# An encoder block on one core: seeded accumulation in two stages of seven-product pairs, normalised-input sums one operation per slot, attention tables in a pool of their own, and new filling counts

## The chip, the core and the metric

The program runs on one core of one Trainium2 chip. The core has a matrix engine (TensorE, "PE" in the profile, with "PEld" for its weight loads), a vector engine (VectorE, "DVE"), an activation engine (ScalarE, "ACT"), GpSimd ("POOL"), and SyncE ("SP"), whose queue here issues the DMAs. Operands lie in SBUF, matrix products accumulate in eight banks of PSUM. The metric is the device time of the program in microseconds; less is better.

## What is computed

The reference is one layer of a hybrid encoder block on 1024 tokens of width 1024, in float32:

```
h = rms_norm(x); proj = h @ w_in            # q,k,v,r, gate codes, swa q,k,v, two branch gates
y_gla = (bidirectional gated linear attention, 4 heads, silu(r) gate) @ w_o_gla
y_swa = (windowed attention, 8 heads, 2 kv heads, rope, sinks) @ w_o_swa
x = x + (sigmoid(gate_a) * y_gla + sigmoid(gate_b) * y_swa) @ w_out
h2 = rms_norm(x); gu = h2 @ w_ffn_in
x = x + (silu(gu[:, :2816]) * gu[:, 2816:]) @ w_ffn_out
```

## The kernel before

Every float32 matrix product is made of three products of rounded operands: a tile is split into a high part (rounded, one ACT operation) and a low part (the rest, one DVE subtraction), and PE runs high x high, high x low and low x high into one bank. The output tiles are 128 x 512, so one "product" of a weight unit (128 x 512) is 4 slices x 3 = 12 matmuls. PE's order is written out by hand (`manual_schedule`); the other engines and the DMA queue are ordered by the compiler's scheduler, on the whole by the order of the program text where operands and buffers are ready.

Dense work that nothing waits for soon is a list of generators, `dense`: the projections of v, q, k (`proj_t`, `proj_f`) and, last in the list, `first_halves`, which makes the first of seven products for twelve pairs of output rows (r, ga and gb, four each). It leaves, for each pair, the product `p1` in DRAM. `fill(n)` takes n matmuls from that list and puts them into PE's order. The stages in between are latency-bound chains, and they run in slots: `slot(stages, n)` issues the stages of one slot with n dense matmuls spread among them. `need(key)` fills on until a projection that a stage reads is done.

- **Linear attention (GLA), slots 0 to 44.** Each slot holds `g_gates` (every other slot), `g_scores`, `g_out`, `g_back_out`, `g_turn` of different chunks. The table `GF` gives n: 34 below slot 8, 21 below 24, 17 below 35, then 10. At the ends of slots 1 to 8, `x_sums` loads tiles of x, normalises them (`x_norm`, line 559) and makes the differences that the second half of the pairs needs (`x_diff`, line 564; `put`, line 116, stores each to DRAM). There are four tiles (`xn`) for these.
- **Windowed attention, slots 0 to 21.** After the pools of GLA are closed, new pools are opened in their place, five tables (cosb, sinb, band, qg, kg) and the sinks are loaded there (line 62 by `load_const`), four tables qA and qB are worked out on DVE (lines 619 to 622), and the slots of `prep`, `a_rope`, `a_scores`, `a_turn`, `k_turn`, `a_out`, `a_probs` run, with n from the table `SF`: 50 below slot 2, 25 below 18, then 15. Line 661 is the load of a key and value tile into the single buffer `kvr`, lines 159 and 167 store and load again the split weights of `proj_t`. Slots 18 to 21 also load and split two parts of the x differences (`xpart`, lines 782, 773, 774).
- **Second half of the pairs.** The last of `dense` is filled in among four `xpart("T2", k)`; then `second_first(0)` (three weight loads, a sum `s1`, its split, the product T1 into the bank Z), eight more `xpart`, and twelve times `second_rest`: products T2, 22, T3, T4 into X and Z. `p1` is loaded (line 869) and added by DVE three times per pair: to Z (line 872, tile p5), to X after T2 (line 877, tile u2), and to X after T4 (in `result`, line 851). Line 830 is a weight load, 835 a weight sum, 821 and 822 the high and low part of a weight.
- **Output projections**, eight-unit groups (`hgroup`), with PE never waiting.
- **Feed-forward, first matrix.** 22 features in `ffn_in`, built like the pairs: `p1` is copied out of PSUM by ACT in `p11`, and added by DVE at line 1106 (p5), 1110 (u2) and 1125 (c21). `between` holds the products of the next feature that stand between T2 and T3.
- **Feed-forward, second matrix** (line 1187), seven products over eleven units with four banks each.

Of the kernel before, what the change touches and what calls it, by code (L numbers as in the profile page):

```python
# [25 lines left out]
GF = ((8, 34), (24, 21), (35, 17), (1 << 30, 10))  # L26
SF = ((2, 50), (18, 25), (1 << 30, 15))
# [5 lines left out]
def body(tc, i, out):  # L33
    nc = tc.nc
    with ExitStack() as root:
# [78 lines left out]
        def put(key, t):  # L114
            d = scratch("_".join(map(str, key)))
            nc.sync.dma_start(out=d, in_=t)
            scr[key] = d

# [435 lines left out]
        part = {}  # L554

# [11 lines left out]
        def x_sums(j):  # L567
            k, late = divmod(j, 2)
            if not late:
                a, b = part[k] = x_norm(k, 0), x_norm(k, 1)  # L570
                x_diff("xT1", k, b, b, a)
                return
            a, b = part.pop(k)
            c = x_norm(k + 4, 1)
            put(("x22", k), c)
            x_diff("xT2", k, b, c, b)
            x_diff("xT3", k, a, b, a)
            c = x_norm(k + 4, 0)
            x_diff("xT4", k, c, c, b)
# [3 lines left out]
        for n in range(NH * NC):  # L583
# [3 lines left out]
            for j, (t, f) in enumerate(((n, g_gates), (n + 2, g_scores), (n + 3, g_out),  # L587
# [3 lines left out]
                last = max(last, t)  # L591
        with tc.manual_schedule(engines={mybir.EngineType.PE}):
            fill(36)
            for t in range(last + 1):
                slot([(lambda v=at[t, j]: v[0](*v[1:])) if (t, j) in at else None for j in (0, 5, 4, 3, 2, 1)], share(GF, t))
                if 1 <= t <= 8:
                    x_sums(t - 1)
# [6 lines left out]
        cosb = load_const(sc_, "cosb", i["c_cos"], (P, KT, 64))  # L604
        sinb = load_const(sc_, "sinb", i["c_sin"], (P, KT, 64))
        band = load_const(sc_, "band", i["c_band"], (P, 384))
        qg = load_const(sc_, "qg", i["qg"], (P, P))
        kg = load_const(sc_, "kg", i["kg"], (P, P))
# [200 lines left out]
        swas.close()  # L809

# [35 lines left out]
        def ntile():  # L846
            return tp.tile([P, HT], F32, tag="nt", name=nm("nt"), bufs=6)
# [8 lines left out]
        def second_first(f):  # L856
            nme, m, a, b = PAIRS[f]
            g = pend[f] = Chunk()
            g.r11, g.r21 = rawload(i["w_f"][a, 0], True), rawload(i["w_f"][b, 0], True)
            g.r22 = rawload(i["w_f"][b, 1], False)  # L860
            g.s1 = comb(g.r21, g.r22, ALU.add)
            g.Z = chtile((P, HT))
            product(g.Z, wsplit(g.s1, 512), XT["T1"], 4, True, False)

        def second_rest(f):
            nme, m, a, b = PAIRS[f]
            g = pend.pop(f)
            p1 = ntile()
            nc.sync.dma_start(out=p1, in_=scr[f"{nme}{m}", "p1"])
            r12 = rawload(i["w_f"][a, 1], False)  # L870
            p5 = ntile()
            nc.vector.tensor_tensor(p5, g.Z, p1, op=ALU.add)
            X = mmtile()
            s2 = comb(g.s1, g.r11, ALU.subtract)
            product(X, wsplit(s2, 512), XT["T2"], 4, True, False)
# [493 lines left out]
```

## Time and profile before

| | |
|---|---|
| median of 3 runs | 1679.72 us (1677.94 to 1680.65) |
| the profiled execution | 1681.57 us, of which 1679.8 us are the span from its first to its last instruction |
| busy share of the span | PE 98%, PEld 81%, DVE 74%, ACT 51%, POOL 0% |
| instructions | 23620, of them 7740 matmuls |
| mean granted clock of PE | 0.993 |
| DMA | 304.32 MB, mean 181 GB/s |

The views used below: the **windows** give, for a stretch of the span, the busy time of each engine with its number of instructions, then the granted clock of PE (1.00 is full), the mean busy share of the DMA engines and GB/s. The **waits** give who waited for whom, with total, number and longest in us. The **groups** give, for a line of code and an operation, the busy time in us, the mean of one in ns, and the idle time of the engine before them with what ended it. The **timeline** gives start, length and, in brackets, the idle time of the engine before and what ended it. `SPq` is the DMA queue of SyncE. The length of a matmul in these rows covers its whole latency; back to back, 512-column matmuls start every 0.227 us (610.06, 610.29, 610.52 in the timeline).

### The profile page before, as it was taken

The page shows a single profiled execution, that of the slowest core. Times are in us where ns is not written, and L with a number is a line of the kernel's source. Part 1 is how long each engine was busy: PE and PEld are TensorE (multiplying, and loading weights), DVE is VectorE, ACT ScalarE, POOL GpSimd, SP SyncE. Part 2 cuts the span into 40 slices and gives each one's busy share as a digit, 9 for nine tenths or more (in the row PEclk, how much of TensorE's full clock was granted, in tenths as well). Part 3 has the DMA queues.
Part 4 walks back from the last instruction along what each step waited for, and adds up shares of the span by engine and source line. Part 5 has one row for each costly group of instructions (what it writes and reads, how often), then busy time and mean ns, then how long its engine had stood idle before and what let it go on. Part 6 is the DMA issues. An engine that isn't in the chain of part 4 may idle for free.

```text
span 1679.8 us, 23620 instructions
## 1 busy us (share of the span) xinstructions
PE 1652.1 (98%) x7740; PEld 1366.0 (81%) x7740; DVE 1250.0 (74%) x2506; ACT 855.2 (51%) x1783; POOL 0.2 (0%) x4
## 2 busy tenths in 40 slices
PE   9989999999999989999999999999999999999999
PEld 7878888887888868888888888788888888888887
DVE  8687887845989777875673668887778877789755
ACT  7445886872897752433553556533333333344443
POOL 0000000000000000000000000000000000000000
PEclk9999999999999999999999999999999999999999
DMA  8875646668654474655764545344224543595533
GB/s 291 292 241 194 213 152 198 220 233 291 202 160 141 126 225 157 225 185 187 237 213 141 192 133 181 114 132 138 89 94 140 165 159 128 178 325 186 150 99 119
DMA packets 185851, 304.32 MB, mean 181 GB/s; under 512 B 21150, under 2 KB 46494, under 8 KB 185728
## 3 DMA queue, kind: packets, MB, share of 16 engines
q1 hardware_dynamic: 185728, 302.81, 55.5%
q8 instruction: 61, 1.00, 0.3%
q14 instruction: 62, 0.51, 0.1%
HBM read 206.26 MB, written 96.47 MB: 180 GB/s over the span
## 4 chain that ended last, share of the span: by engine, by line
PE 81%; DVE 8%; ACT 4%; DMA 4%; issue 2%; SPq 1%; ACTq 0%; DVEq 0%
PE mm L75 25%; PE mm L842 7%; PE mm L843 7%; PE mm L844 7%; PE mm L1187 7%; PE ch L75 6%; PE ch L1187 5%; PE ch L842 4%; PE ch L843 4%; PE ch L844 4%; PE mm L242 3%; PE ch L750 1%; DVE wl L71 1%; DVE cs L418 1%; DMA xr<-in_xT_dram 1%
## 5 line engine op out<-in xcount | busy, mean ns | idle before, releaser
L821 ACT ACTIVATE wh<-ws 128x512 fp32r<-128x512 f32 x136 | 85.5, 632 | 182.5 <-PE mm L843 103.1
L69 ACT ACTIVATE wh<-wr 128x512 fp32r<-128x512 f32 x190 | 118.4, 628 | 103.8 <-PE mm L75 71.3
L71 DVE TENSOR_TENSOR wl<-wr,wh 128x512 fp32r<-128x512 f32 x190 | 129.8, 686 | 26.0 <-ACT wh L69 25.5
L75 PE MATMUL mm<-wh,xh 128*128 128x512 f32 x320 | 128.4, 401 | 1.2 <-DMA wh<-wh 1.1
L75 PE MATMUL mm<-wl,xh 128*128 128x512 f32 x320 | 128.5, 402 | 0.9 <-DMA wl<-wl 0.9
L75 PE MATMUL mm<-wh,xl 128*128 128x512 f32 x320 | 127.7, 399 | 0.0
L822 DVE TENSOR_TENSOR wl<-ws,wh 128x512 fp32r<-128x512 f32 x136 | 93.0, 685 | 12.5 <-ACT wh L821 12.4
L821 ACT ACTIVATE wh<-wr 128x512 fp32r<-128x512 f32 x64 | 40.4, 632 | 114.3 <-issue 47.9
L821 ACT ACTIVATE wh<-a 128x512 fp32r<-128x512 f32 x66 | 41.7, 632 | 92.9 <-PE ch L1187 42.3
L822 DVE TENSOR_TENSOR wl<-a,wh 128x512 fp32r<-128x512 f32 x66 | 45.5, 691 | 41.5 <-ACT wh L821 40.6
L75 PEld LDWEIGHTS mm<-wh,xh 128*128 128x128 f32 x320 | 60.7, 190 | 11.4 <-DMA wh<-wh 1.5
L1187 PE MATMUL mm<-hh,wh 128*128 128x512 f32 x176 | 68.6, 390 | 0.7 <-DVE c L1125 0.7
L75 PEld LDWEIGHTS mm<-wl,xh 128*128 128x128 f32 x320 | 60.7, 190 | 9.9 <-DMA wl<-wl 1.2
L1187 PE MATMUL mm<-hl,wh 128*128 128x512 f32 x176 | 68.5, 389 | 0.0
L1187 PE MATMUL mm<-hh,wl 128*128 128x512 f32 x176 | 68.5, 389 | 0.0
L75 PEld LDWEIGHTS mm<-wh,xl 128*128 128x128 f32 x320 | 60.7, 190 | 9.1
L1160 DVE TENSOR_TENSOR hl<-hr,hh 128x512 fp32r<-128x512 f32 x77 | 52.8, 686 | 3.9 <-ACT hh L1159 3.8
L835 DVE TENSOR_TENSOR ws<-wr,wr 128x512 f32<-128x512 f32 x68 | 46.7, 688 | 8.5 <-DMA wr<-in_w_fi_dram 4.6
L75 PE MATMUL mm<-xh,wh 128*128 128x512 f32 x128 | 51.6, 403 | 0.2 <-ACT wh L69 0.2
L75 PE MATMUL mm<-xl,wh 128*128 128x512 f32 x128 | 51.6, 404 | 0.1
L1187 PE MATMUL ch<-hh,wh 128*128 128x512 f32 x132 | 51.3, 389 | 0.0
L1187 PE MATMUL ch<-hl,wh 128*128 128x512 f32 x132 | 51.3, 389 | 0.0
(546 smaller groups left out, 4986.9 us busy)
## 6 DMA issues: line engine op xcount, KB each, us to landing
wr<-in_w_fi_dram SPq DMA_DIRECT2D x102, 256.0 KB, 2.9
wr<-in_w_f_dram SPq DMA_DIRECT2D x88, 256.0 KB, 3.0
wh<-wh SPq DMA_DIRECT2D x80, 256.0 KB, 2.8
wl<-wl SPq DMA_DIRECT2D x80, 256.0 KB, 3.0
B<-c SPq DMA_DIRECT2D x44, 256.0 KB, 2.1
T<-st SPq DMA_DIRECT2D x44, 256.0 KB, 2.6
a<-in_w_fo_dram SPq DMA_DIRECT2D x44, 256.0 KB, 5.2
hr<-T SPq DMA_DIRECT2D x44, 256.0 KB, 2.6
```

The costliest lines, as they stand in the source:

```text
L69: nc.scalar.activation(h, raw, AF.Copy)
L71: nc.vector.tensor_tensor(l, raw, h.bitcast(F32), op=ALU.subtract)
L75: nc.tensor.matmul(o, a, b, start=start, stop=stop)
L242: nc.tensor.matmul(Y[q], w[:, c], x, start=f0, stop=f1, skip_group_check=True)
L821: nc.scalar.activation(h, src, AF.Copy)
L822: nc.vector.tensor_tensor(l, src, h.bitcast(F32), op=ALU.subtract)
L835: nc.vector.tensor_tensor(t, x, y, op=op)
L842: nc.tensor.matmul(o, h[:, c], x[kk][0], start=start and kk == 0, stop=False, skip_group_check=True)
L843: nc.tensor.matmul(o, h[:, c], x[kk][1], start=False, stop=False, skip_group_check=True)
L844: nc.tensor.matmul(o, l[:, c], x[kk][0], start=False, stop=kk == nk - 1, skip_group_check=True)
L1160: nc.vector.tensor_tensor(l, r, h.bitcast(F32), op=ALU.subtract)
L1187: nc.tensor.matmul(ys[m], a[:, c], b, start=f0, stop=f1, skip_group_check=True)
```

## The change

Six edits, each in the diff below:

1. `GF` has 19 where it had 17 (slots 24 to 34) and 12 where it had 10 (from slot 35). `SF` has 52 for 50 (slots 0 and 1), 24 for 25 (slots 2 to 8), 19 for 25 (slots 9 to 17) and 12 for 15 (slots 18 to 21).
2. `x_sums` is a generator that makes one load with its normalisation, or one difference with its store, at the end of each slot from slot 1 on: 32 steps, done with slot 32.
3. The five tables lie in a pool of their own, `swk`, at the right side of SBUF, opened ahead of GLA and closed after the windowed attention; their loads stand ahead of the slots of GLA. The sinks, qA and qB stay where they were.
4. In the twelve pairs, `p1` is loaded in `second_first` and copied by ACT into the bank X, and T2, T3 and T4 accumulate upon it; T1 goes to a new function `second_go`. What DVE added is now read out by ACT copies: p5 from Z, u2 from X, and the last result from X.
5. `second_first(0)` stands ahead of the third of the four `xpart("T2", k)`, before the last dense matmuls.
6. In the 22 features, `p1` is copied by ACT into X as well; p5 and c21 lose their addition, and u2 is an ACT copy.

```diff
@@ -23,8 +23,8 @@
...
 WARM = 10
-GF = ((8, 34), (24, 21), (35, 17), (1 << 30, 10))
-SF = ((2, 50), (18, 25), (1 << 30, 15))
+GF = ((8, 34), (24, 21), (35, 19), (1 << 30, 12))
+SF = ((2, 52), (9, 24), (18, 19), (1 << 30, 12))
 PAD = 672
@@ -115,6 +115,9 @@
...
             scr[key] = d
+
+        swks = ExitStack()
+        swk = swks.enter_context(tc.tile_pool(name="swk", bufs=1, side="right"))
 
@@ -551,8 +554,6 @@
...
 
-        part = {}
-
         def x_norm(k, s):
@@ -564,19 +565,31 @@
...
 
-        def x_sums(j):
-            k, late = divmod(j, 2)
-            if not late:
-                a, b = part[k] = x_norm(k, 0), x_norm(k, 1)
+        def x_sums():
+            for k in range(KT // 2):
+                a = x_norm(k, 0)
+                yield
+                b = x_norm(k, 1)
+                yield
                 x_diff("xT1", k, b, b, a)
-                return
-            a, b = part.pop(k)
-            c = x_norm(k + 4, 1)
-            put(("x22", k), c)
-            x_diff("xT2", k, b, c, b)
-            x_diff("xT3", k, a, b, a)
-            c = x_norm(k + 4, 0)
-            x_diff("xT4", k, c, c, b)
+                yield
+                c = x_norm(k + 4, 1)
+                put(("x22", k), c)
+                yield
+                x_diff("xT2", k, b, c, b)
+                yield
+                x_diff("xT3", k, a, b, a)
+                yield
+                c = x_norm(k + 4, 0)
+                yield
+                x_diff("xT4", k, c, c, b)
+                yield
+
+        cosb = load_const(swk, "cosb", i["c_cos"], (P, KT, 64))
+        sinb = load_const(swk, "sinb", i["c_sin"], (P, KT, 64))
+        band = load_const(swk, "band", i["c_band"], (P, 384))
+        qg = load_const(swk, "qg", i["qg"], (P, P))
+        kg = load_const(swk, "kg", i["kg"], (P, P))
 
@@ -589,23 +602,19 @@
...
                 last = max(last, t)
+        sums = x_sums()
         with tc.manual_schedule(engines={mybir.EngineType.PE}):
...
                 slot([(lambda v=at[t, j]: v[0](*v[1:])) if (t, j) in at else None for j in (0, 5, 4, 3, 2, 1)], share(GF, t))
-                if 1 <= t <= 8:
-                    x_sums(t - 1)
+                if t:
+                    next(sums, None)
         glas.close()
...
         sw = swas.enter_context(tc.tile_pool(name="swt", bufs=2))
-        cosb = load_const(sc_, "cosb", i["c_cos"], (P, KT, 64))
-        sinb = load_const(sc_, "sinb", i["c_sin"], (P, KT, 64))
-        band = load_const(sc_, "band", i["c_band"], (P, 384))
-        qg = load_const(sc_, "qg", i["qg"], (P, P))
-        kg = load_const(sc_, "kg", i["kg"], (P, P))
         sink = load_const(sc_, "sink", i["sink"], (P, 8))
@@ -807,6 +816,7 @@
...
         swas.close()
+        swks.close()
 
@@ -844,7 +854,7 @@
...
         def ntile():
-            return tp.tile([P, HT], F32, tag="nt", name=nm("nt"), bufs=6)
+            return tp.tile([P, HT], F32, tag="nt", name=nm("nt"), bufs=4)
 
@@ -856,35 +866,44 @@
...
             g = pend[f] = Chunk()
+            p1 = tp.tile([P, HT], F32, tag="np", name=nm("np"), bufs=2)
+            nc.sync.dma_start(out=p1, in_=scr[f"{nme}{m}", "p1"])
+            g.X = mmtile()
+            nc.scalar.copy(g.X, p1)
             g.r11, g.r21 = rawload(i["w_f"][a, 0], True), rawload(i["w_f"][b, 0], True)
...
             g.s1 = comb(g.r21, g.r22, ALU.add)
+            g.w = wsplit(g.s1, 512)
+
+        def second_go(f):
+            g = pend[f]
             g.Z = chtile((P, HT))
-            product(g.Z, wsplit(g.s1, 512), XT["T1"], 4, True, False)
+            product(g.Z, g.w, XT["T1"], 4, True, False)
 
...
             g = pend.pop(f)
-            p1 = ntile()
-            nc.sync.dma_start(out=p1, in_=scr[f"{nme}{m}", "p1"])
+            X = g.X
             r12 = rawload(i["w_f"][a, 1], False)
             p5 = ntile()
-            nc.vector.tensor_tensor(p5, g.Z, p1, op=ALU.add)
-            X = mmtile()
+            nc.scalar.copy(p5, g.Z)
             s2 = comb(g.s1, g.r11, ALU.subtract)
-            product(X, wsplit(s2, 512), XT["T2"], 4, True, False)
+            product(X, wsplit(s2, 512), XT["T2"], 4, False, True)
             u2 = ntile()
-            nc.vector.tensor_tensor(u2, X, p1, op=ALU.add)
+            nc.scalar.copy(u2, X)
             s4 = comb(r12, s2, ALU.subtract)
...
             s3 = comb(g.r11, g.r21, ALU.subtract)
-            product(X, wsplit(s3, 512), XT["T3"], 4, False, False)
+            product(X, wsplit(s3, 512), XT["T3"], 4, False, True)
             result((f"{nme}{m + 4}", 1), X, p5)
...
                 second_first(f + 1)
+                second_go(f + 1)
             product(X, wsplit(g.r22, 512), XT["T4"], 4, False, True)
-            result((f"{nme}{m + 4}", 0), X, p1)
+            t = stage()
+            nc.scalar.copy(t, X)
+            put((f"{nme}{m + 4}", 0), t)
 
@@ -908,10 +927,12 @@
...
             for k in range(4):
+                if k == 2:
+                    second_first(0)
                 xpart("T2", k)
...
             fill(1 << 30)
-            second_first(0)
+            second_go(0)
             for q in ("T3", "T4"):
@@ -1099,19 +1120,19 @@
...
             Z, X = chtile((P, HT)), mmtile()
+            nc.scalar.copy(X, p1)
             s1 = comb(F.r21, F.r22, ALU.add)
...
             nc.scalar.copy(p5, Z)
-            nc.vector.tensor_tensor(p5, p5, p1, op=ALU.add)
             s2 = comb(s1, F.r11, ALU.subtract)
-            product(X, wsplit(s2, 512), YX["T2"], 4, True, False)
+            product(X, wsplit(s2, 512), YX["T2"], 4, False, True)
             u2 = ctile("u2")
-            nc.vector.tensor_tensor(u2, X, p1, op=ALU.add)
+            nc.scalar.copy(u2, X)
             for p, g in between:
...
             s3 = comb(F.r11, F.r21, ALU.subtract)
-            product(X, wsplit(s3, 512), YX["T3"], 4, False, False)
+            product(X, wsplit(s3, 512), YX["T3"], 4, False, True)
             c22 = ctile("c22")
@@ -1122,8 +1143,7 @@
...
             c21, g0 = ctile("c21"), F.g0
-            nc.vector.tensor_tensor(c21, X, p1, op=ALU.add)
-            nc.vector.tensor_tensor(c21, c21, g0, op=ALU.mult)
+            nc.vector.tensor_tensor(c21, X, g0, op=ALU.mult)
             nc.vector.tensor_tensor(c22, c22, u2, op=ALU.mult)
```

## The prediction

> **What bounds the kernel now.** I read the page first, then the windows, the waits of PE stage by stage, and the timeline where PE waits.
>
> ```profile
> PE 1652.1 (98%) x7740; PEld 1366.0 (81%) x7740; DVE 1250.0 (74%) x2506; ACT 855.2 (51%) x1783; POOL 0.2 (0%) x4
> ```
>
> PE is busy for all but 28 us of the span, and no matmul is removed. So the change can gain only where PE waits or runs at a lower clock. The windows say where (span, then busy us of PE, PEld, DVE, ACT, POOL, the granted clock, the share of the DMA engines, GB/s):
>
> ```profile
> 80.00:145.00 65.00, 59.16 (x287) 48.57 (x286) 50.26 (x119) 29.35 (x74) 0.00 (x0) 0.92 0.73 239
> 145.00:260.00 115.00, 114.09 (x662) 97.84 (x661) 94.98 (x270) 88.56 (x255) 0.00 (x0) 1.00 0.56 178
> 260.00:380.00 120.00, 117.20 (x646) 97.10 (x646) 79.29 (x225) 89.00 (x257) 0.00 (x0) 1.00 0.67 223
> 380.00:404.00 24.00, 21.97 (x90) 17.43 (x89) 13.94 (x40) 5.84 (x14) 0.00 (x0) 0.93 0.83 276
> ...
> 477.20:550.50 73.30, 71.71 (x380) 60.56 (x379) 70.45 (x205) 62.60 (x148) 0.00 (x0) 1.00 0.49 154
> 550.50:601.00 50.50, 49.90 (x262) 40.70 (x261) 32.77 (x93) 35.02 (x84) 0.00 (x0) 1.00 0.40 124
> 601.00:627.00 26.00, 19.98 (x78) 15.95 (x77) 20.71 (x33) 15.14 (x26) 0.00 (x0) 0.87 0.84 272
> 627.00:780.00 153.00, 153.00 (x677) 126.60 (x675) 113.73 (x177) 45.84 (x73) 0.00 (x0) 1.00 0.55 183
> ...
> 1076.00:1460.00 384.00, 384.00 (x1695) 318.06 (x1695) 301.77 (x486) 130.86 (x217) 0.00 (x0) 1.00 0.40 131
> ```
>
> Three stretches lose much: the start of GLA (5.84 us idle in 65, and 8% of the clock, 5.2 us), the passage from GLA to the windowed attention (2.03 us, and 7% of 24, 1.7 us), and the passage to the pairs (6.02 us, and 13% of 26, 3.4 us). Together 24 us. In the pairs and the features (627 to 780, 1076 to 1460) PE has no gap, so taking DVE additions away there is worth nothing by itself.
>
> **a. x_sums one operation per slot (80 to 145).** The timeline of DVE at 110, and the groups of the two operations:
>
> ```profile
> 110.83 0.75 DVE L559 SCALAR_TENSOR_TENSOR xn<-xn,g,rstd 128x512 f32<-128x512 f32 x1 [4.12 <-DMA xn<-in_xT_dram]
> ...
> 118.00:124.00 6.00, 3.12 (x13) 1.95 (x12) 6.00 (x16) 3.17 (x9) 0.00 (x0) 0.80 0.31 98
> 124.00:129.00 5.00, 5.00 (x16) 4.09 (x16) 2.58 (x6) 1.66 (x5) 0.00 (x0) 0.56 0.90 289
> L564 DVE TENSOR_TENSOR xn<-xn,xn x16: 669/688/694, 47.0 to 125.5; 128x512 f32<-128x512 f32 x16
> L559 DVE SCALAR_TENSOR_TENSOR xn<-xn,g,rstd x16: 732/748/752, 34.7 to 124.5; 128x512 f32<-128x512 f32 x16
> ```
>
> DVE waits 4.12 us for an x tile, and as it works in order the gates of that slot are late by as much: PE idles 2.88 of the 6 us from 118 and then runs 5 us at 0.56 of its clock. 32 operations (22 us at 0.69 us) with 36 DMAs stand in slots 1 to 8, to about 126 us; now eight stand there. I take 8.5 of the 11.0 us: the residue of 2.5 is more than the next window loses (0.91 in 115), since the slots still hold v's outputs. The ends: 11, and 3 if the DMA waits come back one by one.
>
> **b. The 24 operations that move to slots 9 to 32 (145 to 345).** About 15 of them fall into 145 to 260: 10 us of DVE onto 94.98 of 115, 83% to 91%. Still below full. Nothing if they fill gaps; 10 us if each lies in a gate chain. I take +1.5, nearer to nothing, since DVE has 20 us of gaps there. Their SP work moves with them: 27 of the 36 x-tile DMAs now queue among the loads and stores of these slots, where a store that waits for DVE holds the weight loads behind it; the x loads can run ahead by four buffers.
>
> **c. Two more fills per slot in slots 24 to 44.** 42 matmuls of 0.227 us, in front of stages that leave PE idle for 2.80 us in 260 to 380. That work is not new, it comes from the windowed attention. -1 (from -2.5 to +2, the x operations of slots 24 to 32 included).
>
> **d. Tables early.** The passage at 380:
>
> ```profile
> 384.37 0.43 SPq L661 DMA_DIRECT2D kvr<-skv  x1
> 387.21 0.69 DVE L619 TENSOR_TENSOR qA<-cosb,qg 128x512 f32<-128x512 f32 x1 [11.58 <-DMA kvr<-skv]
> 392.04 0.32 SPq L661 DMA_DIRECT2D kvr<-skv  x1
> 392.40 0.43 SPq L167 DMA_DIRECT2D wh<-wh  x1
> SPq L661 <- DVE qn L636: 3.5, 1, 3.5
> 394.00:398.00 4.00, 1.97 (x8) 1.06 (x8) 4.00 (x7) 0.76 (x3) 0.00 (x0) 1.00 0.97 330
> 398.00:402.00 4.00, 4.00 (x12) 3.15 (x11) 2.97 (x13) 1.74 (x4) 0.00 (x0) 0.57 0.66 224
> ```
>
> The second kvr load waits 3.5 us for DVE to be done with the first tile, and the weight loads of L167 stand behind it in SP's queue; they come too late for PE. With five issues (0.43 us each) gone ahead of the first kvr, and qA and qB worked out before it lands instead of after (four operations, 2.4 us from start to start), the second kvr comes about 4.5 us earlier; PE was short by 2.03. I take -3.5 of 3.7. The sinks stay behind the close of the pools, so the wait for memory stays; if it alone decides, 0. The table loads (5 issues) now stand where PE has 78.52 of 80 us busy at the start; no pool holds them back, and x-tile DMAs leave that stretch by (a). I cost them at nothing; without that cover, up to 2.9 us (0.83 MB at the 292 GB/s of the row below), and this end I keep.
>
> ```profile
> 0.00:80.00 80.00, 78.52 (x357) 61.83 (x358) 61.06 (x114) 48.62 (x86) 0.20 (x4) 1.00 0.86 292
> ```
>
> **e. Fewer fills in the windowed attention.** A 512-column matmul takes 0.227 us from start to start (610.06 and 610.29 under f). From 477 to 550 (slots 9 to 14) DVE is busy 70.45 of 73.30 us: it is as much the bound as PE. Six fills fewer in six slots take 36 x 0.227 = 8.2 us from PE. From DVE they take a split and an output (L71, L245) per 12 matmuls, 3 pairs at 1.2 us by starts, 3.6 us. If DVE keeps its 2.85 us of gaps, the stretch shrinks by 3.6, and 4.6 of the 8.2 us turn into waiting. From 550 on DVE is busy 32.77 of 50.5, and slots 2 to 8 lose one fill each: nothing. +4.6; the ends are 0 and 8.2.
>
> **f. The passage to the pairs.**
>
> ```profile
> L242 PE MATMUL mm<-xh,wh 128*128 128x512 f32 x13 | 5.1, 389 | 0.0
> 610.06 0.39 PE L842 MATMUL ch<-xh,wh 128*128 128x512 f32 x1
> 610.29 0.39 PE L843 MATMUL ch<-xl,wh 128*128 128x512 f32 x1
> 610.98 0.32 SPq L248 DMA_DIRECT2D gb<-st  x1
> 611.58 0.92 SPq L782 DMA_DIRECT2D xn<-xT  x2
> 612.55 0.98 SPq L869 DMA_DIRECT2D nt<-r_p  x1
> 613.59 0.90 SPq L830 DMA_DIRECT2D wr<-in_w_f_dram  x2
> ...
> 619.11 0.69 DVE L835 TENSOR_TENSOR ws<-wr,ws 128x512 f32<-128x512 f32 x1
> 620.48 0.63 ACT L982 ACTIVATE ga<-ga 128x512 f32<-128x512 f32 x1 [2.06 <-DMA ga<-ga]
> 621.68 0.80 PE L842 MATMUL ch<-xh,wh 128*128 128x512 f32 x1 [6.02 <-ACT wh L821]
> ```
>
> After the last attention matmul PE has 3 x 13 = 39 dense matmuls, then T1 and T2; then it waits for the weight s4, whose load (613.59) stands behind the x tiles, `p1`, and the last store of the dense work, and whose split stands behind a gate's sigmoid. By the counts of GF, SF and `need`, slots 20 and 21 and the rest now leave 12 + 12 + 36 = 60. PE has cover for 60 x 0.227 + 24 x 0.227 = 19.1 us after 601, where the split ended about 20.4 us after it (621.0 and 0.6); `p1` is loaded before, and its two additions leave DVE's queue ahead of the sum at 619. (`p1` of every pair is now loaded ahead of the weights of its pair, one load more in front of them at 0.43 us of SP; its bank is taken a product earlier, of four.) I take -7.5 of 9.4. The ends: 9.4, and 0.
>
> **g. Seeds and copies (pairs and features).** Per product pair, DVE loses three additions (0.69 us), ACT gains a seed into PSUM and read-outs: four copies in a pair, two in a feature. No row shows a write into PSUM by ACT; a read from it is
>
> ```profile
> L1105 ACT COPY p<-ch 128x512 f32<-128x512 f32 x22 | 12.5, 567 | 0.0
> L821 ACT ACTIVATE wh<-ws 128x512 fp32r<-128x512 f32 x42 | 26.6, 632 | 65.9 <-PE mm L843 35.2 <-PE ch L843 26.1 <-PE mm L844 2.4
> PE mm L842 <- DVE u L1110: 1.3, 1, 1.3
> ```
>
> I take 0.57 us, the ends 0 and 0.75 (the slowest 128 x 512 row above). ACT has 45.84 us busy of 153 in the pairs and 130.86 of 384 in the features, and four copies add 2.3 us to a pair of 60 x 0.227 = 13.6. Its splits (L821, windows of 627 to 780) wait for PE to free one of five weight buffers, so they run some four products, 10.9 us, ahead: a copy between them costs PE nothing. With that cover gone it would be 0.57 + 0.63 = 1.2 us a pair. The one wait of PE for a DVE read-out, 1.3 us at 1073 behind DVE's queue, goes to an idle ACT: -1.3 (end 0).
>
> **The sum.** -8.5 + 1.5 - 1 - 3.5 + 4.6 - 7.5 - 1.3 = -15.7. The profiled execution took 1681.57 us, 1.77 outside the span; so 1665.9 like for like. It lay 1.85 above the median of the runs, which gives 1664.0 for the median.
>
> One rule against these prices. The Trainium skill, "TensorE: Matmul & The Clock Gate", section "HAM oscillation — how this bites in real kernels", has the clock fall after idle gaps of more than about 3.4 us. By it the gaps of PE before 600 would draw no low clock of their own. The trace disagrees: in 394 to 398 PE was busy 1.97 of 4 us in several pieces, and 0.57 followed.
>
> **The rivals.**
> 1. *The wait for s4 stays.* If the load of s4 still stands behind the last dense store, that store moves later with the 21 more matmuls, and the wait with it. For: 610.98 stands 0.9 us after the last dense matmul. Then f gives 1: 1670.5. Chance 0.15.
> 2. *DVE is the bound in GLA too.* b costs 8, a gives 5: 1674. For: 83% before; against: 20 us of gaps. 0.08.
> 3. *All given back*: b costs 8, e its end of 8.2, f gives 1, the rest as taken: -8.5 + 8 - 1 - 3.5 + 8.2 - 1 - 1.3 = +0.9, 1680.6: no change. The stalls only move to where less filling stands. 0.07.
> 4. *The low clock is not owed to the short gaps* and falls as before: the 5.2 and 1.7 us of a and d stay: 1664.0 + 6.9 = 1671. The rows at 118 and 394, where it follows the gaps, speak against it. 0.04.
> 5. *Slower: ACT's queue.* ACT works in order; if the copy u2, which waits for the end of T2, stands ahead of the split of the weight that PE needs next, PE waits 1.2 us in each of 12 + 22 products: +40.8, 1705. It decides once the lead of the splits falls below one product, 2.7 us. Against: the lead of four. 0.06.
> 6. *All better*: a, d and f whole, e at nothing: 1664.0 - 2.5 - 0.2 - 1.9 - 4.6 = 1655. 0.08.
>
> **How the numbers follow.** The forecast, 1664, has the rest, 0.52. A measurement can tell 0.2% (3.4 us) from no change. Faster: 0.52 + 0.15 + 0.08 + 0.04 + 0.08 = 0.87; same 0.07; slower 0.06. The range from 1653 to 1677 holds the forecast with rivals 1, 2, 4 and 6, and leaves 3 and 5 out.
>
> **What would show it.** a: no wait of DVE for in_xT over 1 us ahead of a gate, and the clock at 1.00 from 80 to 145. b: PE idle below 3 us from 145 to 260. d: no wait of PE for wh or wl of L167. e: in the slots before the end of the attention more waits of PE for DVE (mx, pl), some 4 to 5 us. f: 60 matmuls of L242 behind the last attention product, and a wait for the split of s4 below 2 us. g: no idle PE from the pairs to the end, ACT near 70 of 153 us there. I am wrong if the clock still falls at 100 and 620, or if PE waits for ACT in the pairs.

## The result and the profile after

| | before | after |
|---|---|---|
| median, in the same comparison | 1679.72 us (5 runs) | 1670.45 us (5 runs) |
| ratio, 95% interval | | 0.995 [0.9935, 0.9966] |
| profiled execution, its span | 1681.57, 1679.8 us | 1673.16, 1671.4 us |

The change gains 9.3 us; 15.7 were forecast. Two single runs of the experiments below took far longer than their fellows (2748 and 4250 us) and are left out of the medians. First the page's row of the engines after the change:

```profile
PE 1646.5 (99%) x7740; PEld 1363.1 (82%) x7740; DVE 1190.6 (71%) x2404; ACT 899.4 (54%) x1875; POOL 0.2 (0%) x4
```

DVE lost 59 us of work and ACT took over 44; that by itself shows nothing of the time, since PE stays the bound. Where PE's time went is read in the windows of the changed kernel (columns as before):

```profile
80.00:145.00 65.00, 58.58 (x295) 48.58 (x294) 55.27 (x127) 31.57 (x80) 0.00 (x0) 0.95 0.79 258
145.00:260.00 115.00, 114.09 (x660) 97.68 (x659) 95.01 (x272) 86.90 (x250) 0.00 (x0) 1.00 0.57 183
260.00:380.00 120.00, 118.33 (x655) 99.31 (x655) 78.97 (x222) 86.44 (x253) 0.00 (x0) 1.00 0.69 229
380.00:404.00 24.00, 24.00 (x110) 19.74 (x109) 13.30 (x37) 7.59 (x17) 0.00 (x0) 1.00 0.92 305
...
477.20:550.50 73.30, 72.00 (x386) 60.35 (x384) 70.99 (x214) 60.68 (x146) 0.00 (x0) 1.00 0.39 126
550.50:601.00 50.50, 47.00 (x244) 38.15 (x243) 30.77 (x82) 35.31 (x83) 0.00 (x0) 1.00 0.43 140
601.00:627.00 26.00, 26.00 (x115) 21.18 (x114) 21.52 (x36) 17.27 (x30) 0.00 (x0) 1.00 0.90 303
627.00:780.00 153.00, 149.19 (x650) 122.55 (x649) 89.23 (x137) 63.71 (x111) 0.00 (x0) 0.99 0.52 176
```

The first row has hardly moved, though it was to bring 8.5 us. The two passages, 380 to 404 and 601 to 627, are whole now. And two stretches that lost next to nothing before lose now: 550 to 601 is 3.5 us short, and in the pairs, 627 to 780, PE has gaps and a low clock, though DVE has less work there than ever. Whom PE waits for there, the waits say (total, number, longest, us):

```profile
PE ch L75 <- ACT kth L465: 4.3, 2, 4.0
PE mm L852 <- DVE st L861: 3.8, 2, 2.3
PE ch L75 <- ACT ph L762: 2.3, 1, 2.3
...
PE mm L852 <- DVE c L1137: 1.2, 1, 1.2
```

In the order of the rows these are: the start of GLA, the pairs (L861 is `result`), the last slots of the windowed attention (PE stands from 582 to 584, in slot 19), and the features.

For a common measure, below, I call *loss* of a window its length less PE's busy time, plus its length times what the clock lacks to 1.00. Before, 80 to 145 loses 65 - 59.16 + 65 x 0.08 = 11.0 us. The clock has two digits, so a loss is good to some 0.3 us in 65 us and 0.8 us in 153, and each column is one execution. In us, for before, after, and the experiments told of below (old x: edit 2 undone; no seeds: edits 4 and 6 undone; p1: p1 early, but added by DVE; gate: the gate's sigmoid bound; x: the normalisations bound to their slots; old n: edit 1 undone; then the kernel before with the tables, the counts, or both; last the fastest version):

```
           before  after |  old x  no seeds    p1   gate     x  old n | tables counts  both | fastest
80-145       11.0    9.7 |    8.1       8.6  11.1   10.3   1.6    7.9 |    7.6    7.7   8.8 |     1.6
145-260       0.9    0.9 |    0.9       0.9   0.9    0.9   1.4    0.9 |    0.9    0.9   0.9 |     1.7
260-380       2.8    1.7 |    1.5       1.7   1.6    1.6   3.0    2.8 |    2.8    1.7   1.6 |     2.7
380-404       3.7      0 |      0         0     0      0     0      0 |      0    0.5     0 |       0
404-477       0.7    1.0 |    1.2       1.8   1.1    1.4   1.4    5.7 |    7.2    0.8   1.7 |     1.2
477-550       1.6    1.3 |    1.3       1.3   1.3    1.2   1.5    1.4 |    1.4    1.3   1.3 |     2.2
550-601       0.6    3.5 |    5.0       5.0   3.5    3.5   4.8    0.6 |    0.6    5.1   3.5 |     0.7
601-627       9.4      0 |    0.5       7.4   0.4    0.8   0.5    1.5 |    9.2    4.5   6.6 |     0.3
627-780         0    5.3 |    2.8         0     0    0.4   2.0    4.2 |    0.1      0     0 |       0
1048-1076     1.3    1.2 |    0.6       0.7   3.4    1.0   1.1    1.1 |    1.1    0.4   1.2 |     0.6
```

### The profile page after: what moved, and what is told of

It is laid out like the page before. It is cut to its first block, busy times and chain, and to the rows that moved or that the text cites. A ratio compares the mean times of both kernels' runs of the same rounds, so it can differ in the third digit from the quotient of the medians.

```text
span 1671.4 us, 23580 instructions
## 1 busy us (share of the span) xinstructions
PE 1646.5 (99%) x7740; PEld 1363.1 (82%) x7740; DVE 1190.6 (71%) x2404; ACT 899.4 (54%) x1875; POOL 0.2 (0%) x4
## 4 chain that ended last, share of the span: by engine, by line
PE 83%; DVE 7%; DMA 4%; ACT 3%; issue 2%; SPq 0%; ACTq 0%; DVEq 0%
PE mm L75 28%; PE mm L852 8%; PE mm L853 8%; PE mm L854 8%; PE mm L1207 7%; PE ch L75 6%; PE ch L1207 5%; PE ch L852 3%; PE ch L853 3%; PE ch L854 3%; PE mm L245 3%; DMA vr<-v 1%; DVE wl L71 1%; PE ch L759 1%; DMA wr<-in_w_f_dram 1%
## 5 line engine op out<-in xcount | busy, mean ns | idle before, releaser
L71 DVE TENSOR_TENSOR wl<-wr,wh 128x512 fp32r<-128x512 f32 x190 | 129.5, 685 | 35.7 <-ACT wh L69 35.0
L832 DVE TENSOR_TENSOR wl<-wr,wh 128x512 fp32r<-128x512 f32 x64 | 44.0, 687 | 16.6 <-ACT wh L831 16.5
L845 DVE TENSOR_TENSOR ws<-wr,wr 128x512 f32<-128x512 f32 x68 | 46.5, 687 | 12.5 <-DMA wr<-in_w_fi_dram 8.6
L1179 ACT ACTIVATE hh<-hr 128x512 fp32r<-128x512 f32 x77 | 47.5, 618 | 7.6 <-PE mm L1207 3.9
```

The source lines that it names most:

```text
L71: nc.vector.tensor_tensor(l, raw, h.bitcast(F32), op=ALU.subtract)
L832: nc.vector.tensor_tensor(l, src, h.bitcast(F32), op=ALU.subtract)
L1179: nc.scalar.activation(h, r, AF.Copy)
```

## The experiments

From these rows came a theory with four parts. (1) Edit 2 doesn't place the x operations: only PE's order is written by hand, and the scheduler pulls the rest forward. (2) The counts of edit 1 are what mends the passages. (3) The pairs' new gap comes from the gate loads of `prep_a`, whose sigmoid stands in ACT's queue ahead of splits and copies. (4) The seeds bring nothing but ACT work. The main rivals: edit 2 gains after all, something else hides it; the seeds are what mends 601 to 627; DVE's relief is worth time in the pairs.

### Edit 2 undone: is the spreading worth anything?

```diff
-        def x_sums():
-            for k in range(KT // 2):
-                a = x_norm(k, 0)
-                yield
...
+        def x_sums(j):
+            k, late = divmod(j, 2)
+            if not late:
+                a, b = part[k] = x_norm(k, 0), x_norm(k, 1)
...
-                if t:
-                    next(sums, None)
+                if 1 <= t <= 8:
+                    x_sums(t - 1)
```

> The changed kernel with x_sums as it was (edit 2 undone). If the steps are pulled ahead by the scheduler anyway (the operations end at 133 us in the trace of the changed kernel, 126 us before): within 1.5 us of the changed kernel, 1669 to 1672, and the stall near 93 stays in some form. If the edit does what its text says, as the prediction had it (7 us): 1677.

Measured: 1672.81 us, ratio to before 0.995 [0.9935, 0.9965], the interval of the change itself: 0.8 us above the range expected, and 4 us below the rival's 1677. Undoing the edit costs nothing that can be told. Why, the changed kernel's own rows show, first the group of the normalisations (minimum, median and maximum in ns, first and last start), then the timeline of DVE:

```profile
L560 DVE SCALAR_TENSOR_TENSOR xn<-xn,g,rstd x16: 739/744/754, 34.9 to 132.4; 128x512 f32<-128x512 f32 x16
```

```profile
87.49 0.75 DVE L560 SCALAR_TENSOR_TENSOR xn<-xn,g,rstd 128x512 f32<-128x512 f32 x1 [2.34 <-DMA xn<-in_xT_dram]
```

All sixteen still run from 34.9 to 132.4, where before they ran from 34.7 to 124.5. In the text the last stands at the end of slot 31. Nothing they read comes from their slot, so as soon as a tile and a gap on DVE are there, they go, and DVE still waits for x tiles ahead of gates.

### The normalisations bound to their slots

Part (1) says that spreading would pay if it took place. So the gain `g1` passes through a tiny operation that also reads a value of the current slot's gates (times zero), and the normalisation can't start before it. The values that are computed stay the same.

```diff
+            g = gtile("xg1", (P, 1), bufs=4)
+            nc.vector.scalar_tensor_tensor(g, now[0].sm[:, 0, 0, 0:1], 0.0, g1[:, k:k + 1], op0=ALU.mult, op1=ALU.add)
-            nc.vector.scalar_tensor_tensor(t, t, g1[:, k:k + 1], rstd[:, s * HT:(s + 1) * HT],
-                                           op0=ALU.mult, op1=ALU.mult)
+            nc.vector.scalar_tensor_tensor(t, t, g, rstd[:, s * HT:(s + 1) * HT], op0=ALU.mult, op1=ALU.mult)
...
+                if t % 2 == 0 and t < NH * NC:
+                    now[:] = [gla[divmod(t, NC)].pr]
```

> The changed kernel with each x normalisation bound to its slot: its scale is g1 plus nothing times a value that the gates of that slot produce, one more 128x1 operation on DVE for each of 16. So the 32 operations really spread over slots 1 to 32. By the prediction's price (8.5 gained at 80 to 145, 1.5 lost after it): 1664, PE idle below 3 us from 80 to 145 and the clock at 1.00. If the stalls there do not come from the x operations: 1670. If DVE binds in the later slots: above 1672.

Measured: 1668.55 us, 0.9932 [0.9917, 0.9948]. The windows of this kernel:

```profile
80.00:145.00 65.00, 63.43 (x341) 53.89 (x340) 46.20 (x117) 33.34 (x83) 0.00 (x0) 1.00 0.54 172
145.00:260.00 115.00, 113.63 (x644) 96.33 (x643) 99.34 (x285) 85.26 (x246) 0.00 (x0) 1.00 0.67 218
260.00:380.00 120.00, 117.05 (x650) 98.12 (x649) 81.31 (x232) 86.82 (x254) 0.00 (x0) 1.00 0.77 254
```

The start of GLA has its clock at 1.00 and loses 1.6 us for 9.7: the 8 us that step a forecast are there, but only once the operations really lie in their slots. (The loads of x are spread with them, and the DMA share falls from 0.79 to 0.54; which of the two the stretch gains by is not told apart.) The later slots give 1.8 us back, as step b priced it (1.5). In the whole time less is seen: the median lies between the 1664 and the 1670 of the expectation and moved by 2 us only, with overlapping intervals. The end of the attention lost 1.3 more (a low clock there). And the two executions shown are far apart in their sets: the changed kernel's is 2.7 us above its median, with a mean clock of 0.997 where its other runs had 0.998 or 0.999, and this one 1.6 us below. So the 8 us are the difference of two executions; the medians show 1.9.

### Seeds undone (edits 4 and 6): what does the early load of p1 do?

```diff
-            p1 = tp.tile([P, HT], F32, tag="np", name=nm("np"), bufs=2)
-            nc.sync.dma_start(out=p1, in_=scr[f"{nme}{m}", "p1"])
-            g.X = mmtile()
-            nc.scalar.copy(g.X, p1)
...
+            p1 = ntile()
+            nc.sync.dma_start(out=p1, in_=scr[f"{nme}{m}", "p1"])
...
-            nc.scalar.copy(p5, g.Z)
+            nc.vector.tensor_tensor(p5, g.Z, p1, op=ALU.add)
```

(and so for u2, the last result, and the features)

> The changed kernel with the additions back on DVE, in pairs and features (edits 4 and 6 undone, the rest kept). Theory A (with fewer operations on DVE the gate work of prep_a comes earlier in its queue and waits there for its loads; the results behind it keep PE waiting, 3.8 us and a low clock of 1.7 us at 680 to 720): the additions push it back, PE has no gap from 627 to 780, about 5 us less than the changed kernel, 1665. Theory B (the ACT copies themselves keep PE waiting): the same 1665. Theory C (the stall has come with the earlier start of the pairs): it stays, 1670. In the features both A and B expect no difference, since PE has no gap there in either kernel.

Measured: 1674.41 us, 0.9968 [0.9956, 0.9981]. This missed the 1665 that part (4) gave. The gap in the pairs is gone, as it said, but the passage lost its 7.4 us again. DVE's timeline in this kernel:

```profile
613.42 0.69 DVE L783 TENSOR_TENSOR xl<-xn,xh 128x512 fp32r<-128x512 f32 x1 [3.83 <-ACT xh L782]
614.03 0.68 DVE L886 TENSOR_TENSOR nt<-ch,nt 128x512 f32<-128x512 f32 x1
614.66 0.69 DVE L845 TENSOR_TENSOR ws<-wr,ws 128x512 f32<-128x512 f32 x1
```

L845 is the sum s4. It waits behind the last x tile and p5, and PE waits for its split, though 60 dense matmuls cover the passage as in the changed kernel. The load of its weight is late too. In SP's queue it stands behind the last dense store, which is what rival 1 described:

```profile
608.42 0.32 SPq L251 DMA_DIRECT2D gb<-st  x1
608.78 0.93 SPq L840 DMA_DIRECT2D wr<-in_w_f_dram  x2
```

So the edit bundles two things, the early load of p1 and the accumulation upon it, and the next kernel keeps the first.

### p1 loaded early, but added by DVE in the pairs

```diff
-            p1 = tp.tile([P, HT], F32, tag="np", name=nm("np"), bufs=2)
-            nc.sync.dma_start(out=p1, in_=scr[f"{nme}{m}", "p1"])
-            g.X = mmtile()
-            nc.scalar.copy(g.X, p1)
+            g.p1 = tp.tile([P, HT], F32, tag="np", name=nm("np"), bufs=2)
+            nc.sync.dma_start(out=g.p1, in_=scr[f"{nme}{m}", "p1"])
...
-            nc.scalar.copy(p5, g.Z)
+            nc.vector.tensor_tensor(p5, g.Z, p1, op=ALU.add)
```

> The changed kernel with the additions of the pairs back on DVE (features keep their seeds), but p1 still loaded ahead of the weights of its pair, where the run without seeds loaded it after them and lost 7.5 us again at the passage to the pairs. If the early load of p1 is what made the passage whole: no loss over 1 us at 592 to 627 and no gap in the pairs, 1665 to 1667. If it is that the additions left DVE: the passage loses some 6 us again, as without seeds, 1673 to 1675.

Measured: 1671.24 us, 0.9945 [0.9932, 0.9958]. Windows, and the same sum on DVE:

```profile
601.00:627.00 26.00, 25.59 (x113) 20.74 (x112) 24.38 (x40) 14.28 (x24) 0.00 (x0) 1.00 0.84 273
627.00:780.00 153.00, 153.00 (x676) 126.46 (x675) 110.57 (x174) 46.82 (x75) 0.00 (x0) 1.00 0.58 191
```

```profile
607.90 0.68 DVE L845 TENSOR_TENSOR ws<-wr,ws 128x512 f32<-128x512 f32 x1
```

And the load of its weight in SP's queue:

```profile
603.29 0.43 SPq L840 DMA_DIRECT2D wr<-in_w_f_dram  x1
```

The load goes out 5.5 us earlier, the sum runs at 607.90 instead of 614.66, the passage loses 0.4 us, and the pairs nothing, with DVE back at 110.57 us. So it is the early load, not the accumulation upon p1, that mends the passage, and relieving DVE in the pairs is worth nothing. The whole time did not improve and missed the 1665 to 1667 expected. This execution lost 1.4 us more at the start of GLA and 2.2 more at the features than the changed kernel's, with the same code there. The clock was lower in its other runs too: 0.996 or 0.997 in all five, where the changed kernel's had 0.997 to 0.999. A difference of 0.002 is 3.3 us. Why the clock was lower is open.

### Where the gap in the pairs comes from

ACT's and DVE's timelines in the changed kernel, ahead of the wait at 689:

```profile
683.10 0.63 ACT L922 ACTIVATE sg<-st 128x512 f32<-128x512 f32 x1 [3.19 <-DMA st<-r]
```

```profile
683.76 0.69 DVE L923 TENSOR_TENSOR st<-st,sg 128x512 f32<-128x512 f32 x1 [2.87 <-ACT sg L922]
...
688.10 0.68 DVE L861 TENSOR_TENSOR st<-ch,nt 128x512 f32<-128x512 f32 x1
688.70 0.68 DVE L861 TENSOR_TENSOR st<-mm,nt 128x512 f32<-128x512 f32 x1
```

The sigmoid of `prep_a` waits 3.19 us for its load, and the split behind it on ACT waits too; DVE's gate product waits for the sigmoid, and `result`, which at 688.70 reads the bank that T4 needs, stands behind that product and the rest of the gate work. The first sigmoid of the kernel before, for comparison, in ACT's timeline:

```profile
680.12 0.63 ACT L903 ACTIVATE sg<-st 128x512 f32<-128x512 f32 x1 [0.87 <-DMA st<-r]
```

That is the longest wait of a sigmoid there. After the change the first one runs 12.7 us earlier, at 667.45, in a schedule that now puts these operations ahead of their data. The Trainium skill, "PSUM — Partial Sum Buffer", section "Engine vs sequencer instructions", states that the queues of ScalarE and VectorE are strictly first in, first out; these rows agree, 3.19 us of waiting for a load becomes 2.29 us of PE's.

A first attempt gives these loads other buffers, in which they can start earlier:

```diff
-            o = stage()
+            o, r = (stage() if s else xn.tile([P, HT], F32, tag="xn", name=nm("xn")) for _ in range(2))
...
-            r = stage()
```

> The changed kernel with seeds kept, but prep_a(0, k) loads into tiles of the xn pool, which are free by then, and not into the four st buffers that the results use. Theory A: the loads land before their turn, no wait of ACT for st<-r and no gap of PE from 627 to 780, 1665 to 1666. Theory B: the gaps of PE stay where the copies are, 1670.

Measured: 1672.23 us, 0.9952 [0.9938, 0.9966]: no gain, where 1665 to 1666 was expected. ACT's timeline, and DVE's:

```profile
635.51 0.63 ACT L921 ACTIVATE sg<-xn 128x512 f32<-128x512 f32 x1 [3.31 <-DMA xn<-r]
```

```profile
633.68 0.69 DVE L861 TENSOR_TENSOR st<-mm,nt 128x512 f32<-128x512 f32 x1
```

With buffers free at once, load and sigmoid were both pulled forward by 48 us, and a wait as long stands at 635. The gap of PE moved ahead as well, and shrank: 627 to 780 loses 2.6 us for 5.3, and the longest wait of PE, 1.3 us, ends at 634.42 with the `result` above. In DVE's queue that one stands behind a wait of 3.5 us for a weight and behind the gate work of the first two sigmoids, not behind the wait at 635. So what delays a read-out is gate work ahead of its turn, with or without such a wait; how much of this gap is the weight's is not taken apart. The second attempt binds the use: the loads go out a pair ahead, and the sigmoid takes a bias of zero that is made from u2.

```diff
+                tk = btile1()
+                nc.scalar.activation(tk, u[:, 0:1], AF.Copy, scale=0.0)
+                nc.scalar.activation(sg, r, AF.Sigmoid, bias=tk[:, 0:1])
...
+                u = second_rest(f)
+                for j in range(2):
+                    if 4 <= f < 8:
+                        prep_a(0, 2 * f - 8 + j, gates[2 * f - 8 + j], u)
+                    if 3 <= f < 7:
+                        gates[2 * f - 6 + j] = prep_load(xn, "xn", 0, 2 * f - 6 + j)
```

> The changed kernel with seeds, but the gate work of prep_a(0, k) loads into xn tiles one pair ahead, and its sigmoid is bound to the read-out u2 of its pair (its bias is nothing times a column of u2; one 128x1 ACT copy more, 8 times). So the order on ACT and DVE can't take it before its loads. Theory A (gate work that waits for its loads in the queues of ACT and DVE): no gap of PE over 0.5 us from 627 to 780, 5 us less than the changed kernel, 1665 to 1666. Theory B (the copies fill ACT): gaps of 2 us and more stay near 680 to 720, 1670.

Measured: 1671.66 us, 0.9957 [0.9944, 0.997]. The only wait of PE from 627 to 780 that is left:

```profile
PE mm L852 <- ACT nt L893: 0.4, 1, 0.4
```

The gap is gone with the seeds in place, and the other buffers alone did not remove it. So its cause is the gate work that the scheduler put ahead of its turn, in the changed kernel with the sigmoid's wait, and not the seeds as such. In the time this does not show, against the 1665 expected: the loss in the windows shown is 21 us for 25, the median the same within its spread. The last two kernels have one each of the two cures, and neither has a gap in the pairs.

### Counts and tables, together and apart

The changed kernel with the old counts:

```diff
-GF = ((8, 34), (24, 21), (35, 19), (1 << 30, 12))
-SF = ((2, 52), (9, 24), (18, 19), (1 << 30, 12))
+GF = ((8, 34), (24, 21), (35, 17), (1 << 30, 10))
+SF = ((2, 50), (18, 25), (1 << 30, 15))
```

> The changed kernel with the old GF and SF (edit 1 undone). By the prediction's terms: 1 us lost again at 260 to 380, 3 to 4.6 won at 404 to 592, and at the passage 21 matmuls (4.8 us) less cover: if the seeds and the early loads alone carry it, no loss there, and the sum is 2 to 4 us better, 1667 to 1669; if the counts carry it, 5 us or more lost there, 1672 to 1674.

Measured: 1680.04 us, 1.0002 [0.9992, 1.0012]. The whole gain is gone, and both expectations (1667 to 1669, 1672 to 1674) were too low. Its wait at the start of the attention, and the window there:

```profile
PE ch L75 <- ACT sqh L712: 3.2, 1, 3.2
```

```profile
404.00:424.00 20.00, 16.36 (x81) 13.46 (x79) 16.40 (x61) 11.00 (x28) 0.00 (x0) 0.91 0.74 249
```

404 to 477 loses 4.7 us more than in the changed kernel. Where the rest of the 10 us goes is not shown: over all windows of the table this execution loses only 1.5 us more. The passage to the pairs, though, loses just 1.5 us of 9.4, with the 39 dense matmuls of the kernel before; there the counts are not what mends.

The kernel before with the tables alone (edit 3):

```diff
+        swks = ExitStack()
+        swk = swks.enter_context(tc.tile_pool(name="swk", bufs=1, side="right"))
...
+        cosb = load_const(swk, "cosb", i["c_cos"], (P, KT, 64))
...
-        cosb = load_const(sc_, "cosb", i["c_cos"], (P, KT, 64))
```

> The kernel before with edit 3 alone (tables in their own pool). By the prediction's step d: 3.5 us less than before (of 4.2 lost at 380 to 404), the weight waits of PE there gone, and nothing lost at the start. If the sinks' load alone holds the queue: no difference.

Measured: 1678.81 us, 0.9993 [0.9983, 1.0003]: no change. The windows:

```profile
380.00:404.00 24.00, 24.00 (x111) 19.84 (x110) 15.59 (x43) 7.16 (x15) 0.00 (x0) 1.00 0.89 300
404.00:424.00 20.00, 17.04 (x76) 13.89 (x76) 15.18 (x55) 10.30 (x26) 0.00 (x0) 0.83 0.74 256
```

380 to 404 is whole, just as step d said, and the 3.7 us, with more, are lost 10 us later, where PE waits 2.8 us for the split of the second query tile (sqh). ACT's queue:

```profile
414.01 0.59 ACT L737 ACTIVATE p<-p,nm,rs 128x256 f32<-128x256 f32 x1
...
416.34 0.57 ACT L707 ACTIVATE sqh<-ch 128x512 fp32r<-128x512 f32 x1
```

The split now stands behind the exponentials of the first tile (L737, four from 414.01 on), and ACT is busy up to it. In the kernel before it ran ahead of them, at 419.53, with the exponentials from 420.62 on. So the attention did start earlier (the first split at 401.98 for 408.68, of which 3.4 us come from 80 to 145), and the order on ACT changed with it.

The kernel before with the counts alone (edit 1), and with counts and tables (the diffs are the two above, on the kernel before):

> The kernel before with edit 1 alone (the new GF and SF). My account: 2.5 us won at 260 to 380, nothing at 380 to 404 (its 4 us stay, since the tables are loaded late), 3 to 4 us lost from 404 to 592 to fewer fills, some 2 won at the passage to the pairs (60 fills, but p1 loaded late), no gap in the pairs: 1676 to 1678. Rival: the counts alone carry the gain, since all of it went when they were undone: 1671 to 1673, with the passage to the windowed attention whole.

> The kernel before with edits 1 and 3 (counts and tables). My account: as with the counts alone and 380 to 404 whole besides, without a new stall at 413: 4 us less than the counts alone, 1672 to 1675; what is left against the change is the passage at 600 (5 to 7 us lost there, p1 loaded late), what is better is the pairs (no gap, 6 us). Rival: the stall moves to 413 as it did with the tables alone, then it is equal to the counts alone within 2 us.

Measured: the counts alone 1675.39 us, 0.9977 [0.9968, 0.9986]; both 1674.38 us, 0.9965 [0.9954, 0.9977]. The counts alone lie 4.2 us below before, outside both ranges that were expected, if by 0.6 us from mine. The 1674.38 of both lies in my range, but by luck: the 4 us between the two kernels, on which it rested, did not come, and the difference is the rival's. My account had one thing wrong: 380 to 404 was to keep its 4 us, and it did not, in this window of the counts alone:

```profile
380.00:404.00 24.00, 23.55 (x107) 18.87 (x104) 9.09 (x24) 6.29 (x13) 0.00 (x0) 1.00 0.92 306
```

And SP's queue there:

```profile
393.92 0.73 SPq L167 DMA_DIRECT2D wh<-wh  x1
...
395.24 0.42 SPq L167 DMA_DIRECT2D wl<-wl  x1
395.72 0.98 SPq L655 DMA_DIRECT2D qr<-sq  x2
397.10 0.32 SPq L661 DMA_DIRECT2D kvr<-skv  x1
```

The second kvr load comes at 397.10, 5 us later than before, and yet PE hardly waits, because weight loads now stand ahead of it. So the tables add some 1.0 us between the two medians, which the intervals don't tell from nothing.

### A version that beats both

Now the losses found are taken away together: normalisations bound, p1 early but added by DVE in the pairs, and three matmuls given back to each of the slots that wait for ph, 18 to 21 (the table takes one from each of slots 9 to 17 for it).

```diff
-SF = ((2, 52), (9, 24), (18, 19), (1 << 30, 12))
+SF = ((2, 52), (9, 24), (18, 18), (1 << 30, 15))
```

> The changed kernel with three edits: x's normalisations bound to the gate of their slot, so that they can't run ahead; the pairs' additions of p1 back on DVE with p1 still loaded early; and three of the fills of slots 18 to 21 given back (SF 18 below slot 18, then 15). If the three losses found are apart from one another: -8 + 3 (start of GLA and what follows), -6 (pairs), -2 (the wait for ph at 581): 1659 to 1664. Rival: the losses trade places, as the gate loads did, and it stays at 1666 to 1669, where the bound normalisations alone were.

The twin keeps the seeds and binds the gate's sigmoid:

> The changed kernel with the same bound normalisations and counts, the seeds kept, and the gate loads a pair ahead with the sigmoid bound to u2. Expected as its twin with additions on DVE, 1659 to 1664; by the rival 1666 to 1669. Should the seeds themselves be worth something, it is faster than its twin by over 2 us; I expect no difference.

Measured: 1661.02 us, 0.9892 [0.9876, 0.9909], and 1663.46 us, 0.991 [0.9893, 0.9928]. Both are as forecast, and both lie below the change's interval. Windows of the first:

```profile
80.00:145.00 65.00, 63.44 (x341) 53.92 (x340) 45.48 (x114) 33.23 (x82) 0.00 (x0) 1.00 0.53 173
...
550.50:601.00 50.50, 49.85 (x253) 40.82 (x252) 35.95 (x88) 35.21 (x81) 0.00 (x0) 1.00 0.53 171
601.00:627.00 26.00, 25.75 (x113) 20.70 (x112) 22.02 (x36) 11.13 (x18) 0.00 (x0) 1.00 0.76 256
627.00:780.00 153.00, 153.00 (x676) 126.48 (x675) 110.19 (x173) 49.60 (x83) 0.00 (x0) 1.00 0.57 193
```

The three losses did not trade places this time: the clock stands at 1.00 in all of these windows, and the mean clock of every run of both is 0.999 or 1.000. The twins' intervals overlap, though each of the four runs of the first lies below each of the second, with medians 2.4 us apart. So the seeds in the pairs show no gain; whether they, or the bound gate loads that go with them, cost something is not shown. Which of the three edits brings how much of the step from the change is not taken apart further; bound normalisations alone gave 1668.55.

## Why the prediction was right or wrong

The sign and the range held, with 1670.45 in 1653 to 1677. The point was 6.4 us too low. That the range held is partly luck: steps a and g came out 13.7 us worse than forecast, and b, e and f together 5.1 us better, for reasons that were partly others. The prediction's own sign of being wrong, a clock that still falls at 100, came. In the profiled executions the windows above lose 7.4 us less than before (the span is 8.4 shorter). Of the forecast -15.7, step by step:

- **a, -8.5: wrong.** The step that failed is "now eight stand there". They did not: the operations were placed by text, and nothing held them in place. It measured -1.3, which is no difference that can be told: kernels with the changed code at that place lose 7.9 to 11.1 in the table, those with the old code 7.6 to 11.0. The price is borne out in the windows, where the kernels with bound operations lose 1.6; of one such edit alone the medians show 1.9.
- **b, +1.5: 0**, for the same reason; where they were bound, +1.8 in 145 to 380.
- **c, -1: right**, -1.1, and in every kernel with the new counts and unbound x operations.
- **d, -3.5: the size right (-3.7), the cause not.** The tables alone give that window its 3.7 us back and lose more at 413; the counts alone give 3.2 of it. At d the question of what is late next was not asked: it is the split of the second query tile, behind other work of ACT. So in this change the 3.7 us are the counts', or need them. (The tables are 0.85 MB, not 0.83. That their loads cost the start nothing was right: PE is busy for 78.75 of the first 80 us, before for 78.52.)
- **e, +4.6: the sign, but smaller and in another place.** It is +2.9 over 404 to 601. I put it at slots 9 to 14, where DVE is the bound; these lose no more than before (1.6 to 1.3). It fell into the last slots, 550 to 601, which I had at nothing because DVE has time there: they are chains of latency, and 12 fills don't cover them. With three given back, the loss went to 0.7.
- **f, -7.5: the size right and more**, -9.4, **the cause in part.** The sum was made from the 60 matmuls, and these alone don't do it: the counts alone still lose 4.5, counts and tables 6.6, the change without seeds 7.4. With the early load and 39 matmuls it is 1.5. I named the earlier load of p1 beside the counts; it decides. (It goes with edit 5, which no run leaves out by itself.)
- **g, -1.3: wrong.** In the pairs it is +5.3, at the features -0.1. The step that failed is the pairs at nothing, drawn from "a copy between them costs PE nothing". The copies themselves (0.57 to 0.59 us each) do leave PE without a gap once the gate is bound. But I costed the four copies, and not that the order of the operations around them would change: I looked for cover in the lead of ACT's splits, and a sigmoid of `prep_a` that waits 3.19 us for its load holds up both engines' queues, with the read-out that PE needed behind it. The wait at 1070 only changed its name, to L1137 in the waits above.

Rival 5 had the engine and the in-order queue, but another instruction: not u2 cost time, and not in each pair. Rival 1 did not occur in the whole change, but is part of what the undone seeds show. Rival 3, losses that only move, is what the tables alone do, though there the order on ACT changed and no filling was taken. Rival 4, a low clock not owed to short gaps, is refuted where the gaps went: 380 to 404 and 601 to 627 stand at 1.00.

Still open: why the counts alone set the weight loads ahead of the second kvr, and how much of the 9.3 us is each edit's own; the parts depend on one another, and undoing the counts costs all of it. Added one after the other, the medians give counts 4.2, tables 1.0, edits 4 to 6 with the early p1 some 4, and x_sums 0. Edits 5 and 6 were not tried alone.

## What to carry to other kernels

Where a scheduler orders an engine's queue, as here, moving a line may move nothing unless the operation depends on what stands there: look first whether its inputs are ready long before, and bind it if it must stay. In these kernels an operation that waited for a load held up what stood behind it in its engine's queue, and free buffers let the scheduler pull it in still earlier. A stall that a cover of filler work removes should be tried together with the cover, since apart each may only move it.

## What the hardware showed that was not expected

The low clock is dear beside the gap that draws it. In the change's pairs, one wait of 2.29 us was followed by a clock of 0.68 from 688 to 692 and 0.89 from 692 to 696, 1.7 us more; the wait of 1.52 us at 720 drew none. With the tables alone one wait of 2.8 us (sqh) left 0.83 over 20 us, 3.4 us more. The Trainium skill, "TensorE: Matmul & The Clock Gate", section "HAM oscillation — how this bites in real kernels", has it fall after idle gaps above about 3.4 us; here single waits below 3 us were enough. And at the start of GLA, with the same code, the execution with p1 early had 0.92 with a longest wait of 3.6 us, and the change's own 0.95 with one of 4.0: gaps of the same kind cost 5.2 or 3.3 us.
